# Last pass of a decoder layer's FFN: one token tile in two column halves, Newton steps on GpSimd, VectorE's order fixed

## The chip, the cores and the metric

One core of one Trainium2 chip runs the whole layer as one program. The metric is the device time of one execution in microseconds (us), the median of the runs.

## The reference, cut to what matters

The layer is a hybrid decoder block over 1024 tokens of 1024 channels in float32: attention and a convolution branch are mixed into h, and a convolutional FFN follows. What the change touches is the end of it:

```python
def layer_norm(x, g, b):
    xf = x.astype(jnp.float32)
    mu = xf.mean(-1, keepdims=True)
    var = jnp.square(xf - mu).mean(-1, keepdims=True)
    return ((xf - mu) * lax.rsqrt(var + LN_EPS) * g + b).astype(x.dtype)
...
    up = causal_dwconv(h @ ffn_w_up, ffn_dw, ffn_dw_b)
    u, g = jnp.split(up, 2, axis=-1)
    f = (jax.nn.gelu(g, approximate=False) * u) @ ffn_w_down      # D_FF = 2816 -> 1024
    return layer_norm(DEEPNORM_ALPHA * h + f, ln2_g, ln2_b)
```

## The kernel before

Every float32 product is made of three TensorE products of split operands: high times high, high times low, low times high. The down projection at the end (`f @ ffn_w_down`) is done by a seven-product scheme on 2x2 blocks, so it has seven passes, each a call of `down`: each pass multiplies one sum of blocks of f by one sum of blocks of w_down, for four tiles of 128 tokens by 512 columns, into four banks of PSUM. X and Z name two sets of four banks. A pass runs over the contraction in six `PAIRS` (five of two blocks of 128 and one of one block); a pair is 2 x 3 = 6 products for a token tile (3 for the last). The operands of a pair are loaded, rounded to a high part on ScalarE (line 1659) and given a low part on VectorE (line 1660) ahead of use.

The passes are called in this order; the third argument is what is done with each bank when its products are complete:

```python
    down(X, False, u3)
    down(Z, False, lambda i: add(i, 1, Z[i], full=True))
    down(X, True, c11_, 5)
```

In the last pass `by_tile` is 5: the first pair is multiplied for all four tiles (24 products), and then the other five pairs tile by tile (27 products a tile), so that the tiles end one after the other. For each finished tile `c11_` calls `add` (line 1769: the row tile `r` of 128 x 1024 gets the bank added to its left half, and line 1771 takes the statistics of that half) and `norm_out`: `ln_stats` joins the statistics (line 243), ScalarE gives a first value of 1/sqrt(var + eps) (line 248), three VectorE steps on 128x1 elements improve it (Newton, lines 249 to 251); then for each half of 512 columns, line 1780 forms (r - mean) * g, line 1781 forms that times the 1/sqrt plus b, and SyncE starts the store to `out` (line 112). Both of these read two tiles of SBUF, r and g or r and b.

The names: `r` is a token tile's row, `st` its statistics, `mv` mean and variance, `sd` the pair of 128x1 columns of the Newton steps, `g` and `b` the gain rows. The order of instructions on each engine is set by a scheduler from ranks and a model of time, not by the order of the code; `after(ins, first)` adds an order between two instructions of one engine and no wait. A dependence between engines becomes a semaphore wait, which is kept for PSUM by whole bank.

Of the kernel before, what the change touches and what calls it, by code (L numbers as in the profile page):

```python
# [23 lines left out]
F = mybir.dt.float32  # L24
R = mybir.dt.float32r
AF = mybir.ActivationFunctionType
OP = mybir.AluOpType
AX = mybir.AxisListType

P = 128  # L30
# [18 lines left out]
EPS = 1e-5  # L49
# [14 lines left out]
RK_TURN, RK_SPLIT, RK_EVAC, RK_START, RK_QKV, RK_RESID, RK_ATT = 450, 500, 600, 1000, 10000, 20000, 30000  # L64
# [36 lines left out]
def tile_hybrid_layer(  # L101
# [3 lines left out]
    nc = tc.nc  # L105
# [5 lines left out]
    def load(o, i):  # L111
        return nc.sync.dma_start(out=o, in_=i)
# [8 lines left out]
    def after(ins, first):  # L121

        tc.add_manual_dep(ins.ins, first.ins.name, mybir.DependencyInfo(
            mybir.DependencyClass.NoSync, mybir.DependencyReason.SCHED_ONLY), reason="order of work")

    @contextmanager
    def rank(p):

        saved = tc.cur_priority
        tc.cur_priority = p  # L130
        yield
        tc.cur_priority = saved
# [34 lines left out]
    start = ExitStack()  # L167
# [57 lines left out]
    nc.vector.memset(half_, 0.5)  # L225
    nsink = const.tile([P, NH], F, name="nsink")

    def ln_stats(srcs, pool=None, tag="", bufs=4, behind=None, half_stats=None):

        pool = pool or small  # L230
        J = len(srcs)
        n = max(n for _, n in srcs)
        mv = pool.tile([P, J, 2], F, name="mv", tag="mv" + tag, bufs=bufs)
        if any(m < n for _, m in srcs):
            nc.vector.memset(mv, 1.0)
        for j, (src, m) in enumerate(srcs):
            st = half_stats or small.tile([P, 2, 6], F, name="st")
            for i in range(0 if half_stats is None else 2, 2):
                ins = nc.vector.bn_stats(st[:m, i, :], src[:, i * 512:(i + 1) * 512])
                if behind is not None:  # L240
                    after(ins, behind)
                    behind = None
            nc.vector.bn_aggr(mv[:m, j], st[:m].rearrange("p a b -> p (a b)"))
        sd = pool.tile([P, 2, J], F, name="sd", tag="sd" + tag, bufs=bufs)
        t_, r_ = (sd[:n, i] for i in range(2))
        var = mv[:n, :, 1]

        nc.scalar.activation(r_, var, AF.Abs_reciprocal_sqrt, bias=eps[:n], scale=1.0)
        nc.vector.scalar_tensor_tensor(t_, var, EPS, r_, OP.add, OP.mult)
        nc.vector.scalar_tensor_tensor(t_, t_, -0.5, r_, OP.mult, OP.mult)  # L250
        nc.vector.scalar_tensor_tensor(r_, t_, 1.5, r_, OP.add, OP.mult)
        return [(mv[:m, j, 0:1], r_[:m, j:j + 1]) for j, (_, m) in enumerate(srcs)]
# [24 lines left out]
    def weights(shape, fill):  # L277
        fills[0] += 1
        n = fills[0]
        own = n == 3  # L280
        raw = sp.tile(shape, F, name="wr3") if own else wraw(shape)
        with rank({1: 13, 2: 18, 3: 17, 4: 23}.get(n, RK_SPLIT)):
            last_fill.append(fill(raw))
        hi, lo = (sp.tile(shape, R, name=t + "3") if own else wsp_p.tile(shape, R, name=t, tag=t)
                  for t in ("whi", "wlo"))
        if n <= 3:
            return hi, lo, raw
        with rank(RK_SPLIT):
            last_split.append(split(raw, hi, lo, True))
        return hi, lo  # L290
# [29 lines left out]
    def in_cols(m):  # L320
        return lambda raw: load(raw, w_z[m])
# [161 lines left out]
    first = [weights([P, KC, P], in_cols(m)) for m in (4, 5, 0)]  # L483
# [207 lines left out]
    for r in range(2):  # L691
        rows = slice(r * HD, (r + 1) * HD)
# [60 lines left out]
    for h in range(NH):  # L753
        g, r = divmod(h, 4)
        o = ps[:2, h * 16:(h + 1) * 16]
# [41 lines left out]
    for g in range(NKV):  # L797
        o = po[:, g * 8:g * 8 + 8]
# [21 lines left out]
    for i in range(NB):  # L820
        for g in range(NKV):
# [6 lines left out]
            first = [0, 0] if i else [P, HD]  # L828
            for u in range(2):
# [3 lines left out]
                for h in range(2):  # L833
                    o = ps[:, h * KW:h * KW + w]
                    for j in range(2):
                        nc.tensor.matmul(o, q[:, j, u, h], kflat[:, k0:k0 + w],
                                         start=j == 0, stop=j == 1)
# [13 lines left out]
            hs = slice(g * 4, g * 4 + 4)  # L851
# [3 lines left out]
            for h in range(2):  # L855
                for u in range(2):
                    j = h * 2 + u
                    x = s[:, h, u, first[u]:]
# [91 lines left out]
    def pin(ins):  # L950

        if pinned:
            after(ins, pinned[-1])
        pinned.append(ins)
# [321 lines left out]
    def out_rows(i, between=(), work=()):  # L1276
# [40 lines left out]
        with rank(RK_TURN):  # L1317
            (mu, rs), = ln_stats([(r, n)], half_stats=st if n == P else None)
            for a in (512, 0) if i == 5 else (None,):
                x = r if a is None else r[:, a:a + 512]  # L1320
                ins = pin(nc.vector.tensor_scalar(x, x, mu, rs, OP.subtract, OP.mult))
# [115 lines left out]
    for i in (3, 7, 2, -1, 6, 0, 4, 1, 5):  # L1437
# [3 lines left out]
        rows = out_rows(i, ahead, work.get(i, ()))  # L1441
# [84 lines left out]
    for c in range(FC):  # L1526
# [6 lines left out]
        V4, X, Z, Y = (pup.tile([P, 1024], F, name=n, tag=n) for n in ("pw", "px", "pz", "py"))  # L1533
        passes = ((1,), (0,)) if c == 0 else ((0, 1),)
        for subs in passes:
            last = subs == passes[-1]
            w_next = iter(range(7))
            a, b = SUB[subs[0]][0], SUB[subs[-1]][1]
            i = max(a, 2)

            def at(t, a=a):
                return t[:, 254 + a:254 + b]
# [19 lines left out]
            def tt(*x):  # L1562
                with rank(RK_CHAIN):
                    return nc.vector.tensor_tensor(*x)
# [12 lines left out]
            ins = tt(c11[:, a:b], at(Z), u13[:, a:b], OP.add)  # L1577
# [23 lines left out]
            ins = tt(c22[:, i:b], c22[:, i:b], u13[:, i:b], OP.add)  # L1601
# [20 lines left out]
    dn = ctx.enter_context(tc.tile_pool(name="dn", bufs=1, side="left", reuse_waits="tile"))  # L1622
# [3 lines left out]
    X, Z = ([pd[j] for j in b] for b in ((0, 1, 6, 7), (2, 3, 4, 5)))  # L1626
# [18 lines left out]
    PAIRS = [(j, min(2, FH - j)) for j in range(0, FH, 2)]  # L1645
# [37 lines left out]
    def d_next(ahead=True):  # L1683
        if ahead:
            d_ahead()
        d_taken[0] += 1
        return d_ready.pop(1 if d_taken[0] == EARLY_P else 0)
# [4 lines left out]
    def down(banks, first, done, by_tile=0, same=False):  # L1692


        def mms(i, pairs, a, z):
            ops = [(p, c * 512) for p in pairs for c in range(p[0])]
            for x, ((n, fh, fl, wh, wl), o) in enumerate(ops):
                ts, ws = slice(o + i * P, o + i * P + P), slice(o, o + 512)
                for k, (l, r) in enumerate(((fh, wh), (fh, wl), (fl, wh))):
                    nc.tensor.matmul(banks[i], l[:, ts], r[:, ws], start=first and a and x + k == 0,  # L1700
                                     stop=z and x == len(ops) - 1 and k == 2, skip_group_check=not first)

        n = len(PAIRS) - by_tile
        for y in range(n):
            p = d_next(y < 3 or not same)
            for i in range(4):
                mms(i, [p], y == 0, y == len(PAIRS) - 1)
            if extra:
                extra.pop(0)()
        last = [d_next() for _ in range(by_tile)]  # L1710
        for i in range(4):
            if last:
                mms(i, last, n == 0, True)
            with rank(RK_EVAC):
                ins = done(i)
        if same:
            evacs.append(ins)

    rows, stats = {}, {}
    extra = []  # L1720

    def ln_rows(names):
        return [wsp_p.tile([P, D], F, name=n, tag=t) for n, t in zip(names, ("whi", "wlo"))]

    gains = ln_rows(("g1", "b1"))
# [40 lines left out]
    def add(t, half, bank, op=OP.add, full=False):  # L1766

        r = rows[t][:, half * 512:half * 512 + 512]
        ins = nc.vector.tensor_tensor(r, r, bank, op)
        if full:  # L1770
            nc.vector.bn_stats(stats[t][:, half], r)
        return ins

    def norm_out(t):
        r, (g2, b2_) = rows[t], gains[2:]
        (mu, rs), = ln_stats([(r, P)], half_stats=stats[t])
        for half in range(2):
            hs = slice(half * 512, half * 512 + 512)
            a = r[:, hs]
            nc.vector.scalar_tensor_tensor(a, a, mu, g2[:, hs], OP.subtract, OP.mult)  # L1780
            nc.vector.scalar_tensor_tensor(a, a, rs, b2_[:, hs], OP.mult, OP.add)
            load(out[0, t * P:(t + 1) * P, hs], a)
# [4 lines left out]
        norm_out(4 + i)  # L1787
        return ins

    def c11_(i):  # L1790
        add(i, 0, X[i], full=True)
        norm_out(i)

    down(Z, True, lambda i: add(4 + i, 0, Z[i], OP.subtract))
    down(X, True, lambda i: add(i, 0, X[i]))
    down(Z, True, lambda i: add(4 + i, 1, Z[i]))
    down(X, False, lambda i: add(i, 1, X[i]), same=True)
# [57 lines left out]
```

## Time and profile before

| | |
|---|---|
| median of 3 runs | 1240.19 us (1240.16 to 1240.84) |
| the profiled execution | 1241.21 us, its span 1239.4 us |
| TensorE busy | 1228.1 us, 99% of the span |
| VectorE busy | 1084.9 us, 88% |
| ScalarE busy | 579.6 us, 47% |
| GpSimd busy | 13.3 us, 1% (11 instructions) |
| mean granted TensorE clock | 0.998 |

The span runs from the first to the last instruction; the time of an execution has 1.8 us around it. Times within the profile are us from the span's start. A timeline row gives start, duration, engine, line, operation, output<-input and count; rows of several instructions are merged, with the duration from the first start to the last end. A row of the chain of waits gives start, duration, engine, tile and line.

### The profile page before, as it was taken

How to read it: one execution, taken by the hardware profiler on the slowest of the kernel's cores; microseconds unless marked ns; L12 is line 12 of the kernel's file. 1: busy time of each engine (PE TensorE's matmuls, PEld its weight loads, DVE VectorE, ACT ScalarE, POOL GpSimd, SP SyncE). 2: the span in 40 equal slices, each digit the busy share in tenths (PEclk: the TensorE clock that was granted, in tenths of full speed). 3: DMA queues.
4: the chain of work that ended last, by engine and by line, in shares of the span. 5: the costliest groups of instructions: out<-in, count | busy, mean ns of one | idle time of the engine just before them, and what ended most of it. 6: DMA issues, size and time to landing. Idle time of an engine off the chain costs nothing.

```text
span 1239.4 us, 21709 instructions
## 1 busy us (share of the span) xinstructions
PE 1228.1 (99%) x8545; PEld 1169.1 (94%) x8545; DVE 1084.9 (88%) x1846; ACT 579.6 (47%) x1047; POOL 13.3 (1%) x11
## 2 busy tenths in 40 slices
PE   9999999999999999999999999999999999999997
PEld 8999999999999999888999999999999998888885
DVE  7899989999978798759899999998999986995697
ACT  7522335664255323344755555455454454544330
POOL 0000000000000010000000000000000000000000
PEclk9999999999999999999999999999999999999999
DMA  7296844412264655222145555544455479987722
GB/s 283 67 300 149 194 122 107 122 46 86 80 164 141 177 164 145 102 87 86 52 171 205 204 179 213 184 174 153 162 203 196 174 247 321 387 322 282 255 85 85
DMA packets 109024, 213.08 MB, mean 172 GB/s; under 512 B 31739, under 2 KB 48683, under 8 KB 108794
## 3 DMA queue, kind: packets, MB, share of 16 engines
q1 hardware_dynamic: 93002, 200.63, 49.3%
q10 hardware_dynamic: 15920, 11.07, 3.0%
q8 instruction: 67, 1.10, 0.4%
q14 instruction: 35, 0.29, 0.1%
HBM read 150.04 MB, written 62.70 MB: 172 GB/s over the span
## 4 chain that ended last, share of the span: by engine, by line
PE 96%; DVE 2%; DMA 1%; issue 0%; ACT 0%; SPq 0%; DVEq 0%
PE px L1556 14%; PE py L1556 9%; PE ps_x L1700 9%; PE ps_z L305 8%; PE ps_z L304 8%; PE ps_z L300 8%; PE ps_z L1700 7%; PE pw L1556 5%; PE pz L1556 5%; PE ps_p L300 2%; PE ps_p L304 2%; PE ps_p L305 2%; PE ps_w L305 2%; PE ps_w L304 2%; PE ps_w L300 2%; PE ps_z L514 2%
## 5 line engine op out<-in xcount | busy, mean ns | idle before, releaser
L665 DVE SCALAR_TENSOR_TENSOR FA<-cin,cols,FA 128x1026 f32<-128x1026 f32 x120 | 152.2, 1279 | 0.9
L305 PE MATMUL ps_z<-RHO,wlo 128*128 128x384 f32 (+2 forms) x324 | 104.1, 321 | 0.0
L300 PE MATMUL ps_z<-RHO,whi 128*128 128x384 f32 (+2 forms) x324 | 103.9, 321 | 0.0
L304 PE MATMUL ps_z<-RHO,whi 128*128 128x384 f32 (+2 forms) x324 | 103.9, 321 | 0.0
L305 PE MATMUL ps_z<-RHC,wlo 128*128 128x384 f32 (+2 forms) x324 | 103.8, 320 | 0.0
L304 PE MATMUL ps_z<-RHC,whi 128*128 128x384 f32 (+2 forms) x324 | 103.7, 320 | 0.0
L300 PE MATMUL ps_z<-RHC,whi 128*128 128x384 f32 (+2 forms) x324 | 103.6, 320 | 0.0
L269 ACT CAST whi<-wr 128x1024 fp32r<-128x1024 f32 x37 | 38.9, 1051 | 91.7 <-PE ps_z L304 71.6
L1366 DVE TENSOR_TENSOR RHO<-wr,RHO 128x512 fp32r<-128x512 f32 x92 | 61.9, 685 | 5.2 <-ACT RHO L1365 5.2
L1365 ACT CAST RHO<-wr 128x512 fp32r<-128x512 f32 x92 | 55.3, 619 | 23.3 <-DVE wr L1383 11.4
L300 PEld LDWEIGHTS ps_z<-RHO,whi 128*128 128x128 f32 x324 | 61.0, 188 | 0.1
L300 PEld LDWEIGHTS ps_z<-RHC,whi 128*128 128x128 f32 x324 | 61.1, 189 | 0.0
L304 PEld LDWEIGHTS ps_z<-RHO,whi 128*128 128x128 f32 x324 | 61.0, 188 | 0.0
L305 PEld LDWEIGHTS ps_z<-RHO,wlo 128*128 128x128 f32 x324 | 61.0, 188 | 0.0
L304 PEld LDWEIGHTS ps_z<-RHC,whi 128*128 128x128 f32 x324 | 61.0, 188 | 0.0
L305 PEld LDWEIGHTS ps_z<-RHC,wlo 128*128 128x128 f32 x324 | 61.0, 188 | 0.0
L1383 DVE TENSOR_TENSOR wr<-wr 128x512 f32<-128x512 f32 x88 | 60.2, 684 | 0.2
L272 DVE TENSOR_TENSOR wlo<-wr,whi 128x1024 fp32r<-128x1024 f32 x35 | 42.7, 1219 | 11.5 <-ACT whi L269 11.1
L672 ACT ACTIVATE FA<-ps_z,cols 128x384 f32<-128x384 f32 (+1 forms) x48 | 26.1, 543 | 48.4 <-PE ps_z L305 44.1
L1568 ACT COPY FA<-px 128x514 f32<-128x514 f32 (+2 forms) x23 | 13.1, 571 | 72.1 <-PE px L1556 72.0
L1365 ACT CAST ws<-wr 128x512 fp32r<-128x512 f32 x60 | 36.1, 618 | 19.3 <-DVE wr L1383 10.7
L1556 PE MATMUL px<-OA,RHO 128*128 128x258 f32 (+1 forms) x336 | 43.9, 279 | 0.0
(468 smaller groups left out, 3478.8 us busy)
## 6 DMA issues: line engine op xcount, KB each, us to landing
wr<-in_w_up_dram SPq DMA_DIRECT2D x44, 512.0 KB, 4.9
wr<-in_w_z_dram SPq DMA_DIRECT2D x30, 512.0 KB, 4.4
fd<-FA SPq DMA_DIRECT2D x44, 256.0 KB, 2.4
OB<-in_w_down_dram SPq DMA_DIRECT2D x19, 512.0 KB
qt<-qd SPq DMA_DIRECT2D x28, 256.0 KB, 3.9
sgd<-FA ACTq DMA_DIRECT2D x32, 192.0 KB, 3.0
td<-OB SPq DMA_DIRECT2D x12, 512.0 KB
sums<-fd SPq DMA_DIRECT2D x12, 512.0 KB, 7.0
```

Source lines behind the costliest of these rows:

```text
L269: ins = nc.scalar.copy(hi, raw)
L272: return (nc.vector if quick else nc.gpsimd).tensor_tensor(lo, raw, f32(hi), OP.subtract)
L300: ins = nc.tensor.matmul(ps, ah, bh, start=i == 0, stop=False)
L304: nc.tensor.matmul(ps, ah, bl, start=False, stop=False)
L305: last = nc.tensor.matmul(ps, al, bh, start=False, stop=i == n - 1)
L665: nc.vector.scalar_tensor_tensor(acc[c], cin[:, j:j + U], wc, acc[c], OP.mult, OP.add)
L672: nc.scalar.activation(t, ps, AF.Tanh, bias=bcol(14 + i), scale=0.5)
L1365: nc.scalar.copy(hi, src)
L1366: ins = nc.vector.tensor_tensor(lo, src, f32(hi), OP.subtract)
L1383: ins = nc.vector.tensor_tensor(*x)
L1556: ins = nc.tensor.matmul(o, x[:, ks], bmat(sub, q, hl, k), start=first and k + j == 0, stop=k == 3 and j == 2, skip_group_check=not first)
L1700: nc.tensor.matmul(banks[i], l[:, ts], r[:, ws], start=first and a and x + k == 0, stop=z and x == len(ops) - 1 and k == 2, skip_group_che ...
```

## The change

Three things, all in the last pass (`down(X, True, c11_, 5)`); the six passes ahead of it stand in the same order as before on every engine.

1. The first pair is multiplied for token tiles 0 to 2 only. Tile 3 gets all six pairs at its end, in two column halves: 33 products of 256 columns for columns 0 to 255 of its bank, then 33 for columns 256 to 511 of the same bank. After each half `c11_` adds it and takes its statistics. The statistics of the row's right half, made in the pass before, are copied by GpSimd into the new tile `st3x` of three statistics.
2. The Newton steps of these four tiles run on GpSimd, as five instructions on 128x1 (`pin` branch of `ln_stats`). The first needs the variance alone; the second needs ScalarE's value.
3. `pin_tail` puts VectorE's instructions of the last pass in one order: a tile's add, statistics, join, the two steps with mean and g, the two steps with 1/sqrt and b, and only then the next tile.

```diff
+        if pin:
+            tt, ts, sq = nc.gpsimd.tensor_tensor, nc.gpsimd.tensor_scalar, pool.tile([P, J], F, name="sq")
+            ts(t_, var, EPS, -0.5, OP.add, OP.mult)
+            tt(sq, r_, r_, OP.mult)
+            tt(t_, t_, sq, OP.mult)
+            ts(t_, t_, 1.5, None, OP.add)
+            tt(r_, r_, t_, OP.mult)
+            return [(mv[:m, j, 0:1], r_[:m, j:j + 1]) for j, (_, m) in enumerate(srcs)]
...
-        def mms(i, pairs, a, z):
+        def mms(i, pairs, a, z, cs=slice(0, 512)):
...
-                    nc.tensor.matmul(banks[i], l[:, ts], r[:, ws], start=first and a and x + k == 0,
+                    nc.tensor.matmul(banks[i][:, cs], l[:, ts], r[:, ws], start=first and a and x + k == 0,
...
-            for i in range(4):
+            for i in range(3 if by_tile else 4):
                 mms(i, [p], y == 0, y == len(PAIRS) - 1)
+            if by_tile:
+                held.append(p)
...
         for i in range(4):
-            if last:
+            if last and i == 3:
+                for h in range(2):
+                    mms(i, held + last, True, True, slice(h * 256, h * 256 + 256))
+                    if h == 0:
+                        with rank(RK_EVAC):
+                            done(i, 0)
+            elif last:
                 mms(i, last, n == 0, True)
...
-    def c11_(i):
-        add(i, 0, X[i], full=True)
-        norm_out(i)
+    def c11_(i, part=1):
+        r, (g2, b2_) = rows[i], gains[2:]
+        if i < 3:
+            pieces = [slice(0, 512)]
+        else:
+            pieces = [slice(part * 256, part * 256 + 256)]
+            if part == 0:
+                old, stats[3] = stats[3], dn.tile([P, 3, 6], F, name="st3x")
+                nc.gpsimd.tensor_copy(stats[3][:, 2], old[:, 1])
+        for cs in pieces:
+            pin_tail(nc.vector.tensor_tensor(r[:, cs], r[:, cs], X[i][:, cs], OP.add))
+            pin_tail(nc.vector.bn_stats(stats[i][:, part if i == 3 else 0], r[:, cs]))
+        if i == 3 and part == 0:
+            return
+        (mu, rs), = ln_stats([(r, P)], half_stats=stats[i], pin=pin_tail)
+        halves = [slice(h * 512, h * 512 + 512) for h in range(2)]
+        for hs in halves:
+            pin_tail(nc.vector.scalar_tensor_tensor(r[:, hs], r[:, hs], mu, g2[:, hs], OP.subtract, OP.mult))
+        for hs in halves:
+            pin_tail(nc.vector.scalar_tensor_tensor(r[:, hs], r[:, hs], rs, b2_[:, hs], OP.mult, OP.add))
+            load(out[0, i * P:(i + 1) * P, hs], r[:, hs])
```

What this moves, at the places that the prediction speaks of. First TensorE in the last pass of the kernel before, from its first product to the end of tile 1. `OC`, `RX`, `RHC` and `RHO` hold operands: all products with `OC,RHC` in the first row are the first pair, and a tile's last products are those with `RHO` alone.

```order
L1700 MATMUL ps_x<-OC,RHC 128x512 x24
L1700 MATMUL ps_x<-OC,RX 128x512 x6
L1700 MATMUL ps_x<-OC,RHC 128x512 x6
L1700 MATMUL ps_x<-RHC,RHO 128x512 x12
L1700 MATMUL ps_x<-RHO 128x512
L1700 MATMUL ps_x<-OC,RX 128x512 x6
L1700 MATMUL ps_x<-OC,RHC 128x512 x6
L1700 MATMUL ps_x<-RHC,RHO 128x512 x5
L1700 MATMUL ps_x<-RHO 128x512 x2
L1700 MATMUL ps_x<-RHC,RHO 128x512 x7
L1700 MATMUL ps_x<-RHO 128x512 x3
```

The same place of the changed kernel, TensorE again:

```order
L1710 MATMUL ps_x<-OC,RHC 128x512 x18
L1710 MATMUL ps_x<-OC,RX 128x512 x6
L1710 MATMUL ps_x<-OC,RHC 128x512 x6
L1710 MATMUL ps_x<-RHC,RHO 128x512 x7
L1710 MATMUL ps_x<-OC,RX 128x512 x6
L1710 MATMUL ps_x<-RHC,RHO 128x512 x5
L1710 MATMUL ps_x<-RHO 128x512
L1710 MATMUL ps_x<-OC,RHC 128x512 x6
L1710 MATMUL ps_x<-RHC,RHO 128x512 x11
L1710 MATMUL ps_x<-RHO 128x512 x2
L1710 MATMUL ps_x<-RHC,RHO 128x512
L1710 MATMUL ps_x<-RHO 128x512 x3
```

In both, tile 0's last two products (`RHO` x2) are mixed in among tile 1's, and end as the 67th and 68th product of the pass. Tile 1 now ends with the 72nd and not with the 78th, and tile 2, which has 27 more, with the 99th and not with the 105th.

Next, TensorE's two halves of tile 3 in the changed kernel, with the semaphores that a row waits for:

```order
L1710 MATMUL ps_x<-OC,RHC 128x256 x6
L1710 MATMUL ps_x<-OC,RX 128x256 x6
L1710 MATMUL ps_x<-OC,RHC 128x256 x6
L1710 MATMUL ps_x<-RHC,RHO 128x256 x12
L1710 MATMUL ps_x<-RHO 128x256 x3
L1710 MATMUL ps_x<-OC,RHC 128x256 [waits DVE_49]
L1710 MATMUL ps_x<-OC,RHC 128x256 x5
L1710 MATMUL ps_x<-OC,RX 128x256 x6
```

The first product of the second half has a wait for VectorE that no product of tile 3 had before. The value waited for is the count that VectorE reaches with the add of the first half (line 1825 on 128x256), which reads the same bank.

Last, VectorE in the kernel before, from tile 2's add (`r_11850`; `r_11815` is tile 1) to its last step:

```order
L1769 TENSOR_TENSOR r_11850<-r_11850,ps_x 128x512 [waits PE_49]
L1781 TENSOR_SCALAR r_11815<-r_11815,sd,b_11605 128x512 [waits DVE_49]
L1781 TENSOR_SCALAR r_11815<-r_11815,sd,b_11605 128x512
L1771 BN_STATS st_11851<-r_11850 128x6 [waits DVE_49]
L243 BN_AGGR mv<-st_11851 128x2 [waits DVE_49]
L1780 TENSOR_SCALAR r_11850<-r_11850,mv,g_11604 128x512 [waits DVE_49]
L1780 TENSOR_SCALAR r_11850<-r_11850,mv,g_11604 128x512
L249 TENSOR_SCALAR sd<-mv,sd 128x1 [waits Activation_49]
L250 TENSOR_SCALAR sd<-sd 128x1 [waits DVE_49]
L251 TENSOR_SCALAR sd<-sd 128x1 [waits DVE_49]
L1781 TENSOR_SCALAR r_11850<-r_11850,sd,b_11605 128x512 [waits DVE_49]
L1781 TENSOR_SCALAR r_11850<-r_11850,sd,b_11605 128x512
```

And in the changed kernel, VectorE from tile 2's add to tile 3's join (`r_11885` is tile 3):

```order
L1825 TENSOR_TENSOR r_11850<-r_11850,ps_x 128x512 [waits PE_49]
L1826 BN_STATS st_11851<-r_11850 128x6 [waits DVE_49]
L243 BN_AGGR mv<-st_11851 128x2 [waits DVE_49]
L1832 TENSOR_SCALAR r_11850<-r_11850,mv,g_11604 128x512 [waits DVE_49]
L1832 TENSOR_SCALAR r_11850<-r_11850,mv,g_11604 128x512
L1834 TENSOR_SCALAR r_11850<-r_11850,sd,b_11605 128x512 [waits DVE_49,Pool_49]
L1834 TENSOR_SCALAR r_11850<-r_11850,sd,b_11605 128x512 [waits DVE_49]
L1825 TENSOR_TENSOR r_11885<-r_11885,ps_x 128x256 [waits PE_49]
L1826 BN_STATS st3x<-r_11885 128x6 [waits DVE_49]
L1825 TENSOR_TENSOR r_11885<-r_11885,ps_x 128x256 [waits PE_49]
L1826 BN_STATS st3x<-r_11885 128x6 [waits DVE_49]
L243 BN_AGGR mv<-st3x 128x2 [waits DVE_49]
```

The three Newton rows have left VectorE; a wait for GpSimd (`Pool_49`) stands ahead of a tile's last two steps, and the next tile's add stands behind them. The rows called TENSOR_SCALAR here are SCALAR_TENSOR_TENSOR in the trace.

More of the change, by code (lines that the diff above doesn't have):

```diff
@@ L226, in tile_hybrid_layer, with ln_stats @@
     nsink = const.tile([P, NH], F, name="nsink")
-    def ln_stats(srcs, pool=None, tag="", bufs=4, behind=None, half_stats=None):
+    def ln_stats(srcs, pool=None, tag="", bufs=4, behind=None, half_stats=None, pin=None):
         pool = pool or small
@@ L242, in ln_stats @@
                     behind = None
-            nc.vector.bn_aggr(mv[:m, j], st[:m].rearrange("p a b -> p (a b)"))
+            ins = nc.vector.bn_aggr(mv[:m, j], st[:m].rearrange("p a b -> p (a b)"))
+            if pin:
+                pin(ins)
         sd = pool.tile([P, 2, J], F, name="sd", tag="sd" + tag, bufs=bufs)
@@ L248, in ln_stats @@
         nc.scalar.activation(r_, var, AF.Abs_reciprocal_sqrt, bias=eps[:n], scale=1.0)
+        if pin:
+            tt, ts, sq = nc.gpsimd.tensor_tensor, nc.gpsimd.tensor_scalar, pool.tile([P, J], F, name="sq")
[5 more added lines that the diff above has]
+            return [(mv[:m, j, 0:1], r_[:m, j:j + 1]) for j, (_, m) in enumerate(srcs)]
         nc.vector.scalar_tensor_tensor(t_, var, EPS, r_, OP.add, OP.mult)
@@ L1692, in down @@
     def down(banks, first, done, by_tile=0, same=False):
-        def mms(i, pairs, a, z):
+        def mms(i, pairs, a, z, cs=slice(0, 512)):
             ops = [(p, c * 512) for p in pairs for c in range(p[0])]
             for x, ((n, fh, fl, wh, wl), o) in enumerate(ops):
-                ts, ws = slice(o + i * P, o + i * P + P), slice(o, o + 512)
+                ts, ws = slice(o + i * P, o + i * P + P), slice(o + cs.start, o + cs.stop)
                 for k, (l, r) in enumerate(((fh, wh), (fh, wl), (fl, wh))):
-                    nc.tensor.matmul(banks[i], l[:, ts], r[:, ws], start=first and a and x + k == 0,
+                    nc.tensor.matmul(banks[i][:, cs], l[:, ts], r[:, ws], start=first and a and x + k == 0,
                                      stop=z and x == len(ops) - 1 and k == 2, skip_group_check=not first)
-        n = len(PAIRS) - by_tile
+        n, held = len(PAIRS) - by_tile, []
         for y in range(n):
             p = d_next(y < 3 or not same)
-            for i in range(4):
+            for i in range(3 if by_tile else 4):
                 mms(i, [p], y == 0, y == len(PAIRS) - 1)
+            if by_tile:
+                held.append(p)
             if extra:
@@ L1788, in u3, with pin_tail @@
         return ins
-    def c11_(i):
-        add(i, 0, X[i], full=True)
-        norm_out(i)
+    tail = []
+    def pin_tail(ins):
+        if tail:
+            after(ins, tail[-1])
+        tail.append(ins)
+    def c11_(i, part=1):
[19 more added lines that the diff above has]
+            load(out[0, i * P:(i + 1) * P, hs], r[:, hs])
     down(Z, True, lambda i: add(4 + i, 0, Z[i], OP.subtract))
```

## The prediction

> **What bounds the kernel now.** I read the page first, then the chain of waits over the last 70 us, then the timelines of TensorE, VectorE and GpSimd. The page's chain:
>
> ```profile
> span 1239.4 us, 21709 instructions
> PE 96%; DVE 2%; DMA 1%; issue 0%; ACT 0%; SPq 0%; DVEq 0%
> ```
>
> TensorE carries the program; the change can win or lose only at the end, where the chain passes to VectorE. The chain of waits over that end (rows: start, us, engine, tile, line):
>
> ```profile
> 1201.22 23.82 PE ps_x L1700 x105
> ...
> 1231.28 0.61 DVE r L1769
> ...
> 1231.91 0.70 DVE st L1771
> ...
> 1232.64 0.22 DVE mv L243
> ...
> 1232.88 1.42 DVE r L1780 x2
> 1234.30 0.08 DVE sd L249
> ...
> 1234.40 0.17 DVE sd L250
> ...
> 1234.60 0.17 DVE sd L251
> ...
> 1234.79 0.75 DVE r L1781
> 1235.54 0.66 DVEq L1851
> ```
>
> The last pass starts at 1201.22 and runs at 23.82/105 = 0.227 us a product. Tile 3 costs VectorE 4.92 us, from its add at 1231.28 to 1236.20 (1235.54 + 0.66); 0.49 of it (1234.30 to 1234.79) is the Newton steps. From 1236.20 to the span's end, 3.2 us, lie the last store and the program's close, which the change leaves alone. The timelines of VectorE and of TensorE:
>
> ```profile
> 1216.67 0.69 DVE L1769 TENSOR_TENSOR r<-r,ps_x 128x512 f32<-128x512 f32 x1 [3.74 <-PE ps_x L1700]
> 1225.06 0.69 DVE L1769 TENSOR_TENSOR r<-r,ps_x 128x512 f32<-128x512 f32 x1 [0.58 <-PE ps_x L1700]
> 1216.02 0.62 PE L1700 MATMUL ps_x<-RHO 128*128 128x512 f32 x2
> 1230.30 0.84 PE L1700 MATMUL ps_x<-RHO 128*128 128x512 f32 x3
> ```
>
> Tile 0 reaches VectorE only at 1216.67, since its last two products run at 1216.02 among tile 1's; tile 3's products end at 1231.14. So in these 15 us VectorE has four tiles to finish, and tile 3's add begins (1231.28) when tile 2's last step is done, 0.14 us behind its own products. TensorE and VectorE end level: both are the bound.
>
> **The change part by part.** *256-column products.* A stretch of the up projection has them:
>
> ```profile
> 704.03 1.52 PE L1556 MATMUL py<-RX,ws 128*128 128x256 f32 x12
> 705.39 1.52 PE L1556 MATMUL py<-OC,ws 128*128 128x256 f32 x12
> ```
>
> Twelve take 1.36 us from start to start, 0.113 each, half of 0.227. Two halves of 33 cost what 33 whole products cost: nothing, while TensorE runs on. Tile 2 then ends with the 99th product, at 1201.22 + 99 x 0.227 = 1223.7, and the first half of tile 3 at + 33 x 0.113 = 1227.4. Tile 0's end stays the 68th product, so VectorE starts at 1216.67 as before.
>
> *The new wait.* TensorE's second half waits for VectorE's add of the first half. Behind that wait stand the last 33 products, and behind those VectorE's whole last tile. Ahead of that add VectorE now has three complete tiles, one after another.
>
> *VectorE's three tiles.* A tile without Newton steps costs 1231.28 to 1234.30, 3.02 us, and 1.41 for the last two steps: 4.43. Call w the time that VectorE then waits for GpSimd in each tile. Tile 2 is done at 1216.67 + 3 x 4.43 + 3w = 1229.96 + 3w (TensorE delivers tiles 1 and 2 well before their turn). By itself that is 1.3 us earlier than before, the three stalls saved.
>
> *Tile 3.* The add of 256 columns from PSUM is like this row, where a 258-column step reads one operand from PSUM:
>
> ```profile
> 457.18 0.42 DVE L1141 SCALAR_TENSOR_TENSOR OB<-OB,ps_p 128x258 f32<-128x258 f32 x1
> ```
>
> First half added: 1230.38 + 3w. TensorE restarts (0.1, an estimate), 33 x 0.113 = 3.74, and 0.16 until the last is through (1.52 - 12 x 0.113): 1234.38 + 3w. Then add 0.42, statistics 0.40 (between 0.35, half of 0.70, and 0.70), join 0.24, the two steps with the mean 1.42, w, the last two 1.41: 1238.27 + 4w, against 1236.20. The change costs **2.1 + 4w**. The copy of the old statistics on GpSimd hides behind the 33 products.
>
> *w.* GpSimd does no such step in this trace. Its nearest rows, three memsets and two subtractions of 128x1024:
>
> ```profile
> 0.34 0.10 POOL L1844 MEMSET const-uint8-127<- 128x1 uint8 x1
> 1.73 0.57 POOL L204 MEMSET tab<- 128x572 f32 x1
> 2.36 0.95 POOL L181 MEMSET xm<- 32x1024 f32 x1
> 445.47 2.52 POOL L272 TENSOR_TENSOR RX<-FA,RX 128x1024 fp32r<-128x1024 f32 x1 [442.15 <-DVE OB L1141]
> 456.29 3.24 POOL L272 TENSOR_TENSOR RW<-OB,RW 128x1024 fp32r<-128x1024 f32 x1 [8.30 <-DMA OB<-sgd]
> 1232.88 0.30 ACT L248 ACTIVATE sd<-mv,eps 128x1 f32<-128x1 f32 x1 [4.63 <-DVE mv L243]
> ```
>
> A memset of one element takes 0.10, and a dependent successor starts 0.06 after the end (1.73 + 0.57 to 2.36): 0.16 a step is the low end. The slope of memsets is (0.95 - 0.57)/452 = 0.84 ns an element; taking 1024 of those from 2.52 leaves 1.66 as the far high end of a two-input step. I take 0.30, near the low end, as the steps are one element long but read two operands. After the join VectorE is busy for 1.42. ScalarE's value is there after 0.30, and four dependent GpSimd steps follow: if nothing hindered them, 0.30 + 4 x 0.16 = 0.94 up to 0.30 + 4 x 0.30 = 1.50, and w is about 0. But something does. VectorE around those two subtractions:
>
> ```profile
> 445.28 0.42 DVE L1149 SCALAR_TENSOR_TENSOR RHO<-OB,RHO 128x256 fp32r<-128x256 f32 x1
> 445.62 2.65 DVE L1149 SCALAR_TENSOR_TENSOR RHC<-OB,RHC 128x256 fp32r<-128x256 f32 x1
> 455.99 1.28 DVE L1103 SCALAR_TENSOR_TENSOR two<-FA,pair,two 128x1024 f32<-128x1024 f32 x1
> 457.52 3.09 DVE L1103 SCALAR_TENSOR_TENSOR two<-FA,pair,two 128x1024 f32<-128x1024 f32 x1
> ```
>
> The same step of VectorE, both inputs in SBUF, takes 0.42 alone and 2.65 beside GpSimd's (to 448.27; GpSimd ends at 447.99). The other way round GpSimd's 456.29 began under VectorE's 455.99 and took 3.24 instead of 2.52. The step at 457.18, with one PSUM input, was not held. So GpSimd and a VectorE instruction with two SBUF inputs exclude each other, and both steps with mean and g (line 1780) have two. GpSimd's squaring of ScalarE's value is then caught behind them and starts at about 1.42, so w = 4 x 0.30 + 0.05 = **1.25**; 0.7 at 0.16 a step, 2.45 at 0.6.
>
> The Trainium skill, "SBUF — State Buffer", section "Who interferes with whom", says that a VectorE instruction with two SBUF inputs contends with a GpSimd instruction that reads SBUF, and that the second to issue waits for all of the first. This trace agrees (2.65 against 0.42); by that rule the cost is 2.1 + 4 x 1.25 = 7.1, by the durations alone 2.1.
>
> *The clock.* TensorE now idles from 1227.4 to 1230.4 + 3w = 1234.2, 6.8 us. What an idle TensorE does is seen at the end of this trace (columns: stretch, its length, TensorE busy, granted clock, DMA), and its first products show how it comes back:
>
> ```profile
> 1234.00:1234.50 0.50, 0.00 (x0) 1.00 0.00 0
> 1234.50:1235.00 0.50, 0.00 (x0) 0.75 0.00 0
> 1235.00:1235.50 0.50, 0.00 (x0) 0.50 0.00 0
> 1.08:3.08 2.00, 2.00 (x9) 1.00 0.35 88
> 5.08:7.08 2.00, 2.00 (x17) 1.00 0.86 270
> 7.08:9.08 2.00, 2.00 (x21) 1.00 0.96 379
> ```
>
> The clock fell to 0.50 at about 1234.75, 3.6 us after the last product. At the start products came at 4.5 per us and only after some 4 to 5 us at 10.5, though the clock column does not show it. So the second half starts at half clock: some 4.4 us, 19 products, at 0.227, 0.113 more each: **2.2 us**. Bounds: nothing, and 33 x 0.113 = 3.7.
>
> The Trainium skill, "TensorE: Matmul & The Clock Gate", Part 1, has windows of about 3.4 us that run freely: an idle one halves the clock and a busy one restores it. This trace's 3.6 us agrees; by a return after 3.4 us the term would be 1.7, and a fall can come as late as 6.8 us.
>
> Sum: 2.1 + 5.0 + 2.2 = 9.3 us. The profiled execution took 1241.21 and would take 1250.5; against the median of 1240.19 that is **1249.5**.
>
> **The rivals.**
> - *The clock holds.* If the fall comes later than 3.6 us of idleness, w of 0.5 to 1.25 gives 2.1 + 2 to 5: 1244.3 to 1247.3. For it: one fall in the trace says little on its phase. Against: 6.8 us is nearly twice 3.6.
> - *GpSimd is slower still.* At 0.6 a step w is 2.45: 2.1 + 9.8 + 3 = 14.9, 1255. For it: the far end of 1.66.
> - *Not slower: GpSimd's chain slips under VectorE's steps.* If 128x1 steps get in ahead of or between the two steps of line 1780, and take 0.16, w is about 0; it decides below w = 0.1 ((2.5 - 2.1)/4). Idleness is 3.0, the clock stays, cost 2.1: 1242.3. Against: both subtractions above met the exclusion.
> - *The halves overlap as drawn.* Were TensorE not held by the add, with w = 0, VectorE would get the second half at 1231.1 and end at 1231.1 + 3.9 = 1235.0: 1239.0. Against: the wait stands in the program's order.
>
> **How the numbers follow.** 0.2% is 2.5 us, about what a measurement of this kernel can tell from no change. Forecast 0.57; clock holds 0.18; slow GpSimd 0.13; chain hides 0.08; halves overlap 0.03; 0.01 for a gain over 2.5 us, which no case here gives. Slower: 0.57 + 0.18 + 0.13 = 0.88; same 0.11; faster 0.01. The range starts where the clock holds with w = 0.45, at 1244, and ends at 1254, with w = 1.8 and 3.7 for the clock (2.1 + 7.2 + 3.7 = 13.0) and a little over it; outside are the last cases (0.12) and most of the slow GpSimd (0.08).
>
> **What would show it.** Right: VectorE idle for about 1.25 us ahead of line 1834 in each tile, released by GpSimd; TensorE idle some 7 us between tile 3's halves, released by VectorE's add; a granted clock under 1 and products of 0.23 us in the second half. Wrong: GpSimd's chain ending within 1.4 us of the join, or no gap between the halves.

## The result, and the profile after

The changed kernel takes 1249.12 us (median of 6 runs, 1248.47 to 1250.65), against 1240.31 us before (6 runs, 1239.88 to 1240.84): a ratio of 1.0071, 95% interval 1.0061 to 1.0082. It is 8.8 us slower; 1249.5 was predicted. Its profiled execution took 1249.81 us, 8.60 more than that of before, of which the span has 8.3.

The span on the page of the changed kernel, against 1239.4 before:

```profile
span 1247.7 us, 21791 instructions
```

The chain of waits of the changed kernel over its end (start, us, engine, tile, line):

```profile
1200.74 15.43 PE ps_x L1710 x68
...
1216.20 0.70 DVE r L1825
...
1217.95 0.75 POOL sd L253
...
1220.02 0.20 POOL sd L257
...
1220.24 1.41 DVE r L1834 x2
...
1232.37 0.34 DVE r L1825
...
1232.76 6.73 PE ps_x L1710 x33
...
1243.79 0.66 DVEq L1894
```

The last row, DVEq, is the end of VectorE's last step, booked to its queue. Before, this chain followed TensorE until tile 2 was multiplied (1225.04) and then passed to VectorE once. Now it leaves TensorE 9 us earlier, at tile 0 (1216.17), goes from VectorE to GpSimd and back in each tile, and returns to TensorE only at 1232.76, for the second column half of tile 3. From tile 0's add to the end of the last step it is 28.25 us (1216.20 to 1244.45); before it was 19.53 (1216.67 to 1236.20). I call this stretch the tail and compare kernels by it, since the last pass itself starts up to 1.4 us apart in the profiled executions (TensorE's first row of it stands at 1199.86 in e4 and at 1201.23 in e1). The tail is 8.72 us longer: the whole loss is here.

The waits of the changed kernel from 1200 us on (waiting line, what ended the wait, total, times, longest):

```profile
DVE r L1825 <- PE ps_x L1710: 10.1, 2, 6.3
PE ps_x L1710 <- DVE r L1825: 5.6, 1, 5.6
DVE r L1834 <- POOL sd L257: 3.7, 4, 0.9
```

The two predicted waits are there: TensorE waits once, 5.6 us, for the add of the first half, and VectorE waits in each of four tiles, 0.93 us each, for GpSimd's last step. The 10.1 us at the top are 3.74 us ahead of tile 0, as before, and the 6.35 us in which VectorE waits for the second half. TensorE's rows around the gap, in the timeline of the changed kernel:

```profile
1226.62 0.52 PE L1710 MATMUL ps_x<-RHO 128*128 128x256 f32 x3
1232.76 1.65 PE L1710 MATMUL ps_x<-OC,RHC 128*128 128x256 f32 x6 [5.62 <-DVE r L1825]
```

And the clock in that gap and behind it (stretch, length, TensorE busy with its count, granted clock, DMA share, GB/s):

```profile
1230.00:1231.00 1.00, 0.00 (x0) 1.00 0.00 0
1231.00:1232.00 1.00, 0.00 (x0) 0.83 0.00 0
1232.00:1233.00 1.00, 0.24 (x1) 0.50 0.43 164
...
1237.00:1238.00 1.00, 1.00 (x6) 0.50 0.00 0
1238.00:1239.00 1.00, 1.00 (x9) 0.76 0.00 0
1239.00:1240.00 1.00, 0.47 (x4) 1.00 0.00 0
...
1241.00:1242.00 1.00, 0.00 (x0) 0.95 0.00 0
```

A mean of 0.83 over the second from 1231 puts the fall at about 1231.66, 4.5 us after the last product (1226.62 + 0.52 = 1227.14) and 1.1 us before TensorE restarts. A mean of 0.76 from 1238 puts the return at about 1238.5, 5.7 us after the restart. So 5.7 of the second half's 6.73 us, in which it makes 33 products of 256 columns, ran at half clock. The last row shows the next fall: at 1241.90, 2.4 us after the last product of all (1238.95 + 0.52 = 1239.47).

### The profile page after: what moved, and what is told of

Its sections match the earlier page's. It is cut to its first block, busy times and chain, and to the rows that moved or that the text cites. A ratio compares the mean times of both kernels' runs of the same rounds, so it can differ in the third digit from the quotient of the medians.

```text
span 1247.7 us, 21791 instructions
## 1 busy us (share of the span) xinstructions
PE 1231.3 (99%) x8578; PEld 1173.6 (94%) x8578; DVE 1083.9 (87%) x1836; ACT 579.4 (46%) x1047; POOL 21.2 (2%) x32
## 4 chain that ended last, share of the span: by engine, by line
PE 95%; DVE 2%; DMA 1%; POOL 1%; issue 0%; ACT 0%; SPq 0%; DVEq 0%; POOLq 0%
PE px L1566 14%; PE py L1566 9%; PE ps_x L1710 9%; PE ps_z L314 8%; PE ps_z L315 8%; PE ps_z L310 8%; PE ps_z L1710 7%; PE pw L1566 5%; PE pz L1566 5%; PE ps_p L310 2%; PE ps_p L314 2%; PE ps_p L315 2%; PE ps_w L310 2%; PE ps_w L315 2%; PE ps_w L314 2%; PE ps_z L524 2%
```

## The experiments

All edits are against the changed kernel. Each median is compared with the median of the kernel before on the same chip. The ratios are those on record; for e1 and e4 they differ by 0.0003 from the quotients of the medians. "Tail" is the stretch defined above.

| kernel | median us | before us | difference | ratio, 95% interval | tail us (before 19.53) |
|---|---|---|---|---|---|
| changed kernel | 1249.12 | 1240.31 | +8.81 | 1.0071, 1.0061 to 1.0082 | 28.25 |
| e1 Newton steps on VectorE | 1247.48 | 1240.63 | +6.85 | 1.0052, 1.0035 to 1.0068 | 26.58 |
| e2 whole last tile | 1242.70 | 1240.63 | +2.07 | 1.0015, 1.0006 to 1.0025 | 21.55 |
| e3 second half in another bank | 1243.32 | 1240.63 | +2.69 | 1.0021, 1.0011 to 1.0030 | 21.81 |
| e4 TensorE kept busy in the gap | 1246.97 | 1240.63 | +6.34 | 1.0054, 1.0039 to 1.0069 | 25.76 |
| e5 gain g read from PSUM | 1244.68 | 1240.48 | +4.20 | 1.0033, 1.0021 to 1.0045 | 22.17 |
| e6 VectorE's order alone | 1240.73 | 1240.48 | +0.25 | 1.0003, 0.9994 to 1.0012 | 19.81 |
| e7 two banks, steps in order | 1240.27 | 1240.48 | -0.21 | 0.9998, 0.9989 to 1.0007 | |
| e8 two banks, steps in order, g in PSUM | 1240.20 | 1240.16 | +0.04 | 0.9999, 0.9990 to 1.0008 | |

**e1: halves and order kept, Newton steps back on VectorE.**

```diff
         if pin:
-            tt, ts, sq = nc.gpsimd.tensor_tensor, nc.gpsimd.tensor_scalar, pool.tile([P, J], F, name="sq")
-            ts(t_, var, EPS, -0.5, OP.add, OP.mult)
...
+            stt = nc.vector.scalar_tensor_tensor
+            nsteps.extend((lambda: pin(stt(t_, var, EPS, r_, OP.add, OP.mult)),
...
+        while nsteps:
+            nsteps.pop(0)()
         for hs in halves:
             pin_tail(nc.vector.scalar_tensor_tensor(r[:, hs], r[:, hs], rs, b2_[:, hs], OP.mult, OP.add))
```

> Edit: the changed kernel with the three Newton steps of the last pass back on VectorE, ahead of line 1834; halves and fixed order stay. Theory (each tile pays for GpSimd's chain four times, and TensorE is held by the first half's add): a tile on VectorE costs 4.92 us in place of 5.37, so tile 3's first half is added 1.3 us earlier and TensorE idles about 4.3 us in place of 5.6. If the clock still falls in that time: 1249.1 - 4 x 0.44 = about 1247.3 us; if it holds, 2.8 less: about 1244.5. Rival (GpSimd's steps carry all of the loss): 1240.3.

Without GpSimd's steps TensorE's gap is shorter, but not short enough. Its timeline and the clock windows of e1:

```profile
1227.27 0.52 PE L1710 MATMUL ps_x<-RHO 128*128 128x256 f32 x3
1232.11 1.65 PE L1710 MATMUL ps_x<-OC,RHC 128*128 128x256 f32 x6 [4.33 <-DVE r L1825]
```

```profile
1230.00:1231.00 1.00, 0.00 (x0) 0.99 0.00 0
1231.00:1232.00 1.00, 0.00 (x0) 0.50 0.05 20
```

The clock fell at about 1230.98, some 3.2 us after the last product ended (1227.79), and the second half again began at half clock. The tail is 1.67 us shorter than that of the changed kernel; the wait for GpSimd, 0.93, in place of the same steps on VectorE, 0.49, makes 4 x (0.93 - 0.49) = 1.76. The halves, with the clock that they lose and VectorE's fixed order, cost the rest, 7.05 us of tail.

**e2: the last tile whole, GpSimd's steps and the order kept.**

```diff
-            for i in range(3 if by_tile else 4):
+            for i in range(4):
                 mms(i, [p], y == 0, y == len(PAIRS) - 1)
...
-            if last and i == 3:
...
+            if last:
                 mms(i, last, n == 0, True)
...
+        pieces = [slice(0, 512)]
```

> Edit: the changed kernel without the halves; tile 3 is multiplied in products of 512 columns as before, its first pair with the others; Newton on GpSimd and the fixed order stay. Theory: no wait of TensorE for VectorE, so neither idleness nor a lower clock; VectorE is the bound with four tiles of 5.37 us from 1216.2, against 4.92 at the most before: about 2.0 us over before, 1242.3 us. Rival (the order or GpSimd carries the loss): 1249.

VectorE's last step in the timeline of e2:

```profile
1235.99 1.42 DVE L1820 SCALAR_TENSOR_TENSOR r<-r,sd,b 128x512 f32<-128x512 f32 x2 [0.93 <-POOL sd L257]
```

The median is 0.4 us above the expected one. VectorE's waits are those of the changed kernel, four of 0.92 to 0.93, and the tail is 2.02 us longer than before: 4 x (0.93 - 0.49) = 1.76, and 0.28 that the fixed order takes alone (e6). Of the three edits GpSimd's steps cost 2 us and the halves the greater part; the two sum up, 7.05 from e1 and the 1.76, to 8.8.

**e3: the second half goes to another PSUM bank.** TensorE then has no reason to wait for the add of the first half.

```diff
-                    mms(i, held + last, True, True, slice(h * 256, h * 256 + 256))
+                    mms(i, held + last, True, True, slice(h * 256, h * 256 + 256), Z[3] if h else None)
...
-            pin_tail(nc.vector.tensor_tensor(r[:, cs], r[:, cs], X[i][:, cs], OP.add))
+            pin_tail(nc.vector.tensor_tensor(r[:, cs], r[:, cs], (Z[3] if i == 3 and part else X[i])[:, cs], OP.add))
```

> Edit: the changed kernel with the second half of tile 3 in another bank (the fourth of the Z set, free since the pass before), so that its products need not wait for the first half's add. Everything else stays. Theory: TensorE ends at 1230.7 and VectorE is the bound: tile 2 done at 1232.3, both halves' adds and statistics 1.75, the rest of tile 3 4.1: about 6.4 us less than the changed kernel, 1242.7 us, with a granted clock as before. Rival (halves cost by themselves, by twice the products): no gain, 1249.

TensorE's timeline and VectorE's of e3:

```profile
1226.97 0.88 PE L1711 MATMUL ps_z<-OC,RHC 128*128 128x256 f32 x6
...
1230.57 0.52 PE L1711 MATMUL ps_z<-RHO 128*128 128x256 f32 x3
```

```profile
1232.28 0.41 DVE L1826 TENSOR_TENSOR r<-r,ps_x 128x256 f32<-128x256 f32 x1
1233.07 0.40 DVE L1826 TENSOR_TENSOR r<-r,ps_z 128x256 f32<-128x256 f32 x1
...
1236.58 1.42 DVE L1835 SCALAR_TENSOR_TENSOR r<-r,sd,b 128x512 f32<-128x512 f32 x2 [0.93 <-POOL sd L257]
```

The gap is gone: the second half follows the first at once and its products end at 1231.09. But VectorE, with a wait of 0.93 us in each tile, adds the first half only at 1232.28 and the second at 1233.07, both long after their products. The median is 0.6 us above the expected one. So 6.1 us of the 8.8, the lower clock among them, come from both halves sharing a bank, and 2.7 us remain that the halves can't win back, as VectorE is by then the bound. The wait is one that the program sets for a whole bank; whether the halves of one bank could do without it was not tried.

**e4: TensorE multiplies on through the gap.** Behind the first half stand 22 products of 512 columns, into a bank that nothing reads afterwards.

```diff
                         with rank(RK_EVAC):
                             done(i, 0)
+                        fh, wh = last[0][1], last[0][3]
+                        for _ in range(22):
+                            nc.tensor.matmul(Z[0], fh[:, :P], wh[:, :512], start=True, stop=True)
```

> Edit: the changed kernel with 22 products of 512 columns added between the two halves of tile 3, into a bank that nobody reads (22 x 0.227 = 5.0 us of extra work in the idle stretch). The wait for VectorE stays. Theory (the lower clock costs 2.8 us of the second half): TensorE idles under 1 us, the clock holds, and the second half takes 3.9 in place of 6.7 us: 1249.1 - 2.8 = 1246.3 us although 22 products more are done. Rival (the clock record says nothing on speed; the second half is slow for another cause): 1249.1 or more.

TensorE's timeline of e4, and its clock in the second half and behind it:

```profile
1226.26 5.18 PE L1732 MATMUL ps_z<-OC,RX 128*128 128x512 f32 x22
1232.04 0.98 PE L1710 MATMUL ps_x<-OC,RHC 128*128 128x256 f32 x6 [0.61 <-DVE r L1828]
...
1235.73 0.52 PE L1710 MATMUL ps_x<-RHO 128*128 128x256 f32 x3
```

```profile
1232.00:1234.00 2.00, 1.96 (x16) 1.00 0.63 237
...
1238.00:1240.00 2.00, 0.00 (x0) 0.65 0.00 0
```

The second half took 4.2 us (1232.04 to 1236.25) instead of 6.73, at full clock, with the wait for the add still there. The tail is 2.49 us shorter, the median 2.47. That is the price of the clock, measured with the order, the wait and the Newton steps left alone; the median is still 0.7 us above the expected one. The last row puts the fall at the end of the program at 1238.60, 2.35 us after the last product (1236.25).

**e5: g, the gain, is read from PSUM.** ScalarE copies it ahead of the last pass into two banks that are free by then, so that the two steps of line 1832 have one operand in SBUF and one in PSUM.

```diff
-        for hs in halves:
-            pin_tail(nc.vector.scalar_tensor_tensor(r[:, hs], r[:, hs], mu, g2[:, hs], OP.subtract, OP.mult))
+        for h, hs in enumerate(halves):
+            pin_tail(nc.vector.scalar_tensor_tensor(r[:, hs], r[:, hs], mu, Z[h], OP.subtract, OP.mult))
...
+    with rank(RK_EVAC):
+        for h in range(2):
+            nc.scalar.copy(Z[h], gains[2][:, h * 512:h * 512 + 512])
     down(X, True, c11_, 5)
```

> Edit: the changed kernel with the gain row g copied by ScalarE into two free banks of PSUM before the last pass, so that the two steps with mean and g (line 1832) read one operand from SBUF and one from PSUM. Theory (VectorE instructions with two SBUF inputs keep GpSimd's steps out): the first GpSimd step takes about 0.2 us in place of 0.75 and the second 0.2 in place of 0.59, the chain ends about 1.5 us after the join, VectorE waits 0.1 in place of 0.93 in each tile, 3.3 us less in all; TensorE idles some 3.1 us in place of 5.6, and if that is too short for the clock to fall another 2.8 go: 1243.0 us (1245.8 if it falls all the same). Rival (these two steps are slow by themselves): waits as they are, 1249.1.

GpSimd's steps for tile 0 in the timeline of the changed kernel, and then in that of e5:

```profile
1217.95 0.75 POOL L253 TENSOR_SCALAR sd<-mv 128x1 f32<-128x1 f32 x1 [5.14 <-DVE mv L243]
1218.78 0.59 POOL L254 TENSOR_TENSOR sq<-sd 128x1 f32<-128x1 f32 x1
1219.44 0.19 POOL L255 TENSOR_TENSOR sd<-sd,sq 128x1 f32<-128x1 f32 x1
1219.72 0.21 POOL L256 TENSOR_SCALAR sd<-sd 128x1 f32<-128x1 f32 x1
1220.02 0.20 POOL L257 TENSOR_TENSOR sd<-sd 128x1 f32<-128x1 f32 x1
```

```profile
1218.38 0.19 POOL L253 TENSOR_SCALAR sd<-mv 128x1 f32<-128x1 f32 x1 [5.13 <-DVE mv L243]
1218.70 0.19 POOL L254 TENSOR_TENSOR sq<-sd 128x1 f32<-128x1 f32 x1
...
1219.55 0.19 POOL L257 TENSOR_TENSOR sd<-sd 128x1 f32<-128x1 f32 x1
```

VectorE's timeline of the changed kernel, and then of e5:

```profile
1217.89 1.42 DVE L1832 SCALAR_TENSOR_TENSOR r<-r,mv,g 128x512 f32<-128x512 f32 x2
1220.24 1.41 DVE L1834 SCALAR_TENSOR_TENSOR r<-r,sd,b 128x512 f32<-128x512 f32 x2 [0.93 <-POOL sd L257]
```

```profile
1218.32 1.41 DVE L1832 SCALAR_TENSOR_TENSOR r<-r,mv,ps_z 128x512 f32<-128x512 f32 x2
1219.78 1.41 DVE L1834 SCALAR_TENSOR_TENSOR r<-r,sd,b 128x512 f32<-128x512 f32 x2
```

The same GpSimd instruction takes 0.75 beside a VectorE step with two SBUF operands and 0.19 beside one that reads PSUM. In the changed kernel the first step spans all of VectorE's first step of line 1832, the squaring all of the second. In e5 nothing is held; the chain of five ends at 1219.74, level with line 1832 (1219.73), and in place of the wait of 0.93 stand 0.05. The Trainium skill, "SBUF — State Buffer", section "Who interferes with whom", says that a VectorE instruction with two SBUF inputs contends with a GpSimd instruction that reads SBUF, and one with at most one such input does not; these rows agree with it. TensorE's gap is then 2.94 us, and the clock windows of the profiled execution of e5 show no fall in it:

```profile
1228.00:1230.00 2.00, 0.00 (x0) 1.00 0.00 0
1230.00:1232.00 2.00, 1.49 (x12) 1.00 0.70 262
```

Its tail is 2.64 us longer than before: what the halves in one bank still cost with w near zero and the clock held. The time missed its expectation by 1.7 us. The two profiled executions are 2.97 us apart (1244.18 and 1241.21), as the tail has it, but the medians are 4.20 apart. The profiled execution is the fastest of the five, and its mean granted clock is 0.999; the other four, 0.45 to 0.87 us slower, have 0.997 to 0.998. A thousandth of 1242 us is 2.5 us at half clock, so this points to a clock that did fall in their gap, but the mean clock of the kernel before also varies between 0.998 and 0.999, and no trace shows those four: it stays open.

**e6: VectorE's fixed order alone.** Whole last tile (as e2) and Newton steps on VectorE (as e1).

> Edit: of the change only VectorE's fixed order; tile 3 whole, Newton steps on VectorE. Theory: VectorE works without a gap from tile 0 on, four tiles of 4.92 us, as it nearly did before: the same within 0.2% (before plus 0.1 us). Rival (the order itself costs, since nothing fills the waits for ScalarE and the Newton steps): 1 to 2 us more.

The add of tile 3 in the timeline of e6, and then in that of the kernel before:

```profile
1230.88 0.68 DVE L1813 TENSOR_TENSOR r<-r,ps_x 128x512 f32<-128x512 f32 x1
```

```profile
1231.20 0.68 DVE L1769 TENSOR_TENSOR r<-r,ps_x 128x512 f32<-128x512 f32 x1
```

No difference that can be told: +0.25 us, interval 0.9994 to 1.0012. A tile takes 4.93 us in it (1216.08 to 1230.88 in three), against 4.84 before (1216.67 to 1231.20 in three).

**e7: the halves as they could have been.** Two banks; the first half's products of the early pairs multiplied together with the other tiles; TensorE held to the written order from tile to tile; and the Newton steps on VectorE between pieces of the step with mean and g, so that each finds its operand ready.

```diff
+                    if by_tile and x + k == 0 and mm_last:
+                        after(ins, mm_last[-1])
+            mm_last.append(ins)
...
+                if by_tile and i == 3:
+                    mms(i, [p], True, False, slice(0, 256))
...
-                    mms(i, held + last, True, True, slice(h * 256, h * 256 + 256))
+                    mms(i, (held if h else []) + last, h == 1, True, slice(h * 256, h * 256 + 256), Z[3] if h else None)
...
-        for hs in halves:
+        for hs in (slice(0, 512), slice(512, 768), slice(768, 1024)):
             pin_tail(nc.vector.scalar_tensor_tensor(r[:, hs], r[:, hs], mu, g2[:, hs], OP.subtract, OP.mult))
+            nsteps.pop(0)()
```

> Edit: a version meant to end earlier than before: halves of tile 3 in two banks (no wait of TensorE), the first half's first pair done early, TensorE's products of the last pass pinned tile by tile so that tile 0 ends as about the 48th product in place of the 68th, Newton on VectorE between pieces of the steps with mean and g. Theory: VectorE starts tile 0 some 3.7 us earlier and waits for TensorE at tile 3; after TensorE's end there remain an add and statistics of 256 columns, the join, the four steps and a shorter Newton, 4.3 us in place of 5.06: 0.7 us under before, a ratio of 0.9994. Rival (VectorE or the low parts of the last operands hold it elsewhere): the same as before or more.

TensorE's and VectorE's timelines of e7:

```profile
1230.25 0.52 PE L1711 MATMUL ps_z<-RHO 128*128 128x256 f32 x3
```

```profile
1230.81 0.42 DVE L1832 TENSOR_TENSOR r<-r,ps_z 128x256 f32<-128x256 f32 x1 [1.50 <-PE ps_z L1711]
...
1233.86 1.42 DVE L1842 SCALAR_TENSOR_TENSOR r<-r,sd,b 128x512 f32<-128x512 f32 x2
```

Now VectorE waits for TensorE again, and its last step ends 4.51 us behind the last product (1230.77 to 1235.28), where it took 5.06 before (1231.14 to 1236.20). So the halves, with the Newton steps out of the way, do win 0.55 us behind TensorE once nothing holds it. In the time it is not to be told from no change (0.9998, 0.9989 to 1.0007); 0.7 us less were expected.

**e8: TensorE as in e7, g in PSUM as in e5, Newton steps on GpSimd, the copy of the statistics on ScalarE.**

```diff
-                nc.gpsimd.tensor_copy(stats[3][:, 2], old[:, 1])
+                nc.scalar.copy(stats[3][:, 2], old[:, 1])
```

> Edit: the version in two banks and pinned tile by tile, with the Newton steps on GpSimd again and g in PSUM, so that GpSimd's chain runs beside the two steps with mean and g; the copy of the old statistics is on ScalarE. Theory: behind TensorE's end stand an add and statistics of 256 columns 0.85, the join 0.27, two steps 1.42, a wait under 0.1, two steps 1.41: 4.0 us in place of 5.06, so 1.0 us under before, 1239.5 us, a ratio of 0.9992. The time around the span was 2.1 to 2.2 us in the four kernels that had both the copy and the Newton steps on GpSimd, 1.8 in the others; if the copy makes it, it is 1.8 here, and if GpSimd beside the halves makes it, 2.15 and the gain is 0.7. Rival (the end is held elsewhere): the same as before.

TensorE's and VectorE's timelines of e8:

```profile
1226.59 0.88 PE L1711 MATMUL ps_z<-OC,RHC 128*128 128x256 f32 x6
1227.31 0.88 PE L1711 MATMUL ps_z<-OC,RX 128*128 128x256 f32 x6
...
1230.19 0.52 PE L1711 MATMUL ps_z<-RHO 128*128 128x256 f32 x3
```

```profile
1233.45 1.42 DVE L1841 SCALAR_TENSOR_TENSOR r<-r,sd,b 128x512 f32<-128x512 f32 x2
```

Behind the last product (1230.71) VectorE needs 4.16 us, 0.9 less than before. But six products of 256 columns take 0.72 from start to start, 0.120 each and not 0.113: 66 of them take 7.92 us where 33 whole ones took 33 x 0.227 = 7.49. By this 0.4 of the 0.9 go back to TensorE, and the 0.5 that would be left, 0.04%, lies inside the interval. 1.0 us less were expected. Neither e7 nor e8 is shown to beat the kernel before.

## Why the prediction was right, step by step

- **The bound, and the new wait: right.** TensorE and VectorE ended level before. The add of the first half now holds TensorE, behind three whole tiles of VectorE: 5.62 us idle (6.8 predicted; most of the difference is 3 x 0.32 of w, below, and the first half's longer products are the rest). e3, which takes away only the reason for the wait, wins 6.1 us back.
- **A tile without Newton steps, 4.43 + w: right.** The adds of the changed kernel at 1216.20 and 1232.29 are three tiles apart, 5.36 each, and 5.36 - 0.93 = 4.43.
- **w: right mechanism, size 0.93 and not 1.25.** The pitch of a step was right: 0.29 from start to start (1219.44, 1219.72, 1220.02) against 0.30. That is partly luck: 0.30 was chosen between 0.16 and 1.66, and the 0.06 behind the 0.16 was read between two memsets of different tiles, which do not depend on each other. Wrong was that the squaring would wait out *both* steps of line 1832 and leave four steps behind them. GpSimd gets through once between the two steps: the first instruction ends with the first, the squaring with the second (1218.78 + 0.59 = 1219.37, against 1217.89 + 1.42 = 1219.31), and three steps are left: 3 x 0.29 + 0.06 = 0.93. Four tiles: 3.7, not 5.0. That the exclusion causes it, and not slow GpSimd steps, is shown by e5.
- **The clock: right, 2.5 and not 2.2.** It fell inside the gap and came back later than assumed, 5.7 us after the restart instead of 4.4. e4 gives the price by itself: 2.49 us of tail. How long TensorE had idled says little on when the clock falls: in the gaps it fell 3.2 us (e1) and 4.5 us (changed kernel) after the last product, at the programs' ends between 2.1 us (e8, 1230.71 to 1232.79) and 5.0 us (e7, 1230.77 to 1235.76; clock windows of 0.25 us). The pitch says more: in the changed kernel from the fall to the return are 6.8 us (1231.66 to 1238.48), and from there to the next fall 3.4 (1241.90). The Trainium skill, "TensorE: Matmul & The Clock Gate", Part 1, has windows of about 3.4 us that run freely, of which an idle one halves the clock and a busy one restores it. These distances, two windows and one, agree with it, and so does the return, which came only after a window that TensorE filled from end to end. The falls after 2.1 to 2.4 us do not agree with a window that must be idle throughout, and the measurement decides.
- **Products of 256 columns "cost nothing": slightly wrong.** 0.120 and not 0.113 here. From the end of the add to the end of the half are 4.27 us in e5 (1230.46 to 1234.73), not 0.1 + 3.74 + 0.16 = 4.0; the restart itself took 0.05. This is the larger part of why the rest of the sum, 2.1, was 2.5: by subtraction 8.72 - 3.7 - 2.5 = 2.5 in the changed kernel, and 2.64 measured in e5, where w is 0.05 and the clock holds.
- **The sum.** 2.1 + 5.0 + 2.2 = 9.3 was predicted; 2.5 + 3.7 + 2.5 = 8.7 is what the tail shows, and 0.3 more lies around the span (2.1 us in place of 1.8), which no term had. The total came out close because w was taken too high by 1.3 and the other terms too low by 0.7, with 0.3 unforeseen: the agreement to 0.4 us is partly luck, the order of the terms is not.
- **The rivals.** The clock did not hold; GpSimd's pitch was not 0.6. The chain did not slip under VectorE's steps, though it does as soon as g is in PSUM (e5), which is where that rival's condition lay. The halves did not overlap as drawn; e3 shows that overlap alone would not have been enough, since four waits of 0.93 us had made VectorE the bound, and e7 and e8, which have no such waits, are not shown to gain either.

## What to carry to other kernels

When the two engines at a program's end are level, an edit that makes the first wait for the second puts the second's whole queue into the first's path: list what stands ahead of the awaited instruction before splitting a tile, and give the two parts a bank each. A gap in TensorE's work can have a second price, the half-speed restart: 2.5 us here behind a gap of 5.62. A gap of 2.94 us (e5) was free of it in the execution that was profiled, but that is no safe length: at the end of e8 the clock fell after 2.1 us without a product. Small steps moved to GpSimd were free here only where the VectorE work that was to hide them did not read two operands from SBUF (e5), and they are worth moving only if the engine that gains is still the bound afterwards.

## What was not expected of the hardware

- Between two VectorE steps with two SBUF operands, issued back to back, one waiting GpSimd instruction gets through and the next is caught by the second step: 0.75 and 0.59 us for instructions that otherwise take 0.19.
- After a gap of 5.62 us the clock stayed at 0.50 for 5.7 us of dense products. Falls came 2.1 to 5.0 us after a last product.
- The same products of 256 columns take 0.120 us each in the last pass and 0.113 in the up projection; no run tells why.
- The time around the span is 2.10 to 2.20 us where the page counts 32 instructions on GpSimd (the changed kernel, e3, e4, e5) and 1.74 to 1.86 where it counts 31 or fewer (before, e1, e2, e6, e7, e8). e2 and e8 have the Newton steps on GpSimd but not the copy of the statistics. That the count itself is the cause was not tried.
